# A two-layer trunk kernel: squares of the output projection as tasks of their own, reloads issued in pairs, one table load placed earlier

## The chip, the cores and the metric

The kernel runs on one core of one Trainium2 chip. The metric is the device time of one execution in microseconds (us), as the median of several runs; lower is better. TensorE is called PE here (its weight loads PEld), VectorE DVE, ScalarE ACT, GpSimd POOL and SyncE SP, as in the profile.

## The reference, cut to what matters

Two groups of tokens (128 of context, 512 latent, together T = 640) go through two layers and a closing norm. Each layer normalizes its input, projects it, mixes it in two branches, gates the result, and projects it back with a residual:

```python
for l in range(DEPTH):                      # DEPTH = 2
    shift, scale, gate = modulation(c, ada_w[l], ada_b[l])
    h = rms_norm(x, norm_g[l]) * (1.0 + scale) + shift
    y, side = even_mixer(h, ...) if l % 2 == 0 else odd_mixer(h, ...)
    x = x + gate * (y @ w_out[l])           # the output projection, 2048 x 2048
y_out = rms_norm(x, final_norm_g)           # the closing norm
```

`rms_norm` divides by the root of the mean of `x * x` over the 2048 features. The change is about these squares of the new `x`: their sum over the features is needed by the next layer's norm and by the closing norm.

## The kernel before, in words

**Layout.** Features lie on partitions: `x` is 16 tiles of 128 features by 640 tokens. A projection makes one such tile (a chunk) at a time, in two banks of PSUM (columns 0 to 319 and 320 to 639), with 16 steps over the input features.

**Products in three parts.** Full float32 precision is put together from reduced operands: every input tile is kept as `acth` + `actl`, every weight as `whi` + `wlo`, and PE does whi*acth, whi*actl and wlo*acth (L757). The split of the weights runs while PE works: SP loads raw weights (`wload`, L640), ACT copies them to `whi` (L714), POOL subtracts to get `wlo` (L716; DVE takes every second unit of the last pair of chunks, L715). `whi` and `wlo` are rings of 2560 columns, so a split waits until PE has left the room. `wpump` (L655) emits these steps.

**Strassen pairs.** Most chunks are done two at a time (`spair`, L870) with seven products over six pairs of input tiles and a plain rest. The raw weights come into `rs`, sums of them (S1, S2, S4, S3) are made by DVE into `wraw` and `rs`, and the products run in the order A11, plain, A12, S1, S2, S4, plain, S3, A22 (L596). PE meets the pieces as `acth` or `eh` operands. Folded input sums (`eh`, `el`) and a rewritten half of six `acth`/`actl` tiles serve these products; `unfold` (L1130) reloads the old halves from DRAM (`bh_dram`, `bl_dram`) once a run of Strassen pairs ends, and raises a flag `uf0` to `uf5` for each tile.

**The order of the work** is written by a planner: `Pace` models when each engine would be free; `tick` (L482) is called every few matmuls, emits due DMAs (`dmas`), up to three steps of `wpump`, and advances a list of generator tasks in their order, by default one step a call. A task yields a time, or waits for flags (`wait`), for data in the model (`until`) or until engines' modelled backlog is small (`calm`). `need` moves the model's clock forward by 0.4 us a round until flags are there. All of it fixes only the order in which instructions enter each engine's queue; on the chip an engine runs its queue in order and waits on semaphores.

**The output projection** (`out_proj`, L2409) is done once a layer (l = 0 and 1): chunks n = 0 and 1 as an ordinary pair, n = 2 to 13 as six Strassen pairs, n = 14 and 15 as an ordinary pair (l = 0, `kpair`) or as the closing pair (l = 1, `hpair`, L843, which does columns 0 to 383 of both chunks first, half 0, then columns 384 to 639, half 1). `out_evac` (L1969) takes a finished bank: DVE computes `Y <- bank * G + x` (L1999), and `square` (L1973) then calls `ssq_add` (L1240): ACT squares the half tile into a small buffer, POOL adds that to the running sum `ssq`:

```python
            sq = sq[:, : c.stop - c.start]
            nc.scalar.activation(sq, x[:, c], AF.Square)                      # L1246
            nc.gpsimd.tensor_tensor(ssq[:, c], ssq[:, c], sq, ALU.add)        # L1247
```

In the profile these are `ACT arena<-Y 128x320` and `POOL arena<-arena 128x320`, because `ssq` and the buffers lie in the tile `arena`. The weight splits show as `whi<-rs`, `whi<-wraw`, `wlo<-rs` and `wlo<-wraw`.

**The end.** Before the closing pair a task `reload` (L2638) is started; after `unfold` it reads four pairs of finished output tiles back from DRAM. `final` (L2646) runs after each half of the closing pair: PE sums `ssq` and the last squares over partitions, `rms` (L1220) does Ln and Exp on ACT, DVE finishes the factor, and 16 tiles are scaled and stored, by DVE and, for five of them, by ACT and POOL. Ln and Exp need another ACT table set than the SiLU of the gates; `act` calls `tables` (L524) ahead of the first Ln, and this gives the `ACT_TABLE_LOAD` of L526.

Of the kernel before, what the change touches and what calls it, by code (L numbers as in the profile page):

```python
# [13 lines left out]
AF = mybir.ActivationFunctionType  # L14
ALU = mybir.AluOpType
# [4 lines left out]
KT = D // 128  # L20
# [15 lines left out]
NY = 8  # L36
# [203 lines left out]
class Trunk:  # L240
# [889 lines left out]
    def unfold(self):  # L1130

        nc = self.nc
        for i, j in enumerate(JT):
            for x, y in zip((self.ah, self.al), self.keep):
                self.dma(x[:, j, CW:].bitcast(U32), y[:, j, :].bitcast(U32))
                yield
            self.flags.add(f"uf{i}")
        self.flags.add("unfold")
        self.folded = False
        yield  # L1140
# [828 lines left out]
    def out_evac(self, l, n, f, xsrc, spill):  # L1969
        nc = self.nc  # L1970
        box = {}

        def square(y, c):  # L1973
            if l == 1 and f == KT - 1:
                nc.scalar.activation(self.sq[:, : c.stop - c.start], y[:, c], AF.Square)
            else:
                self.ssq_add(self.ssq, y, f, self.sq if self.cut == CUT else self.sqs.next(), c)

        def squares(y):
            if n == KT - 1:  # L1980
                yield from self.wait("squares")
            for q, s in ((slice(0, HT), self.sqs.next()), (slice(HT, T), self.sqs.next())):
                yield from self.wait("x1:14")
                yield from self.calm(2.0, "a")
                nc.scalar.activation(s, y[:, q], AF.Square)
                yield from self.until(s)
                yield from self.calm(4.0, "v")
                nc.vector.tensor_tensor(self.ssq[:, q], self.ssq[:, q], s, ALU.add)
                yield
            self.flags.add("squares")  # L1990

        def evac(pa, pb):
            G, at = self.G[l], self.cut
            y = self.Y[:, n % NY, :]
            if pa is not None:
                if n < NY:
                    self.clear(f"Y{n}", "C", "R")
                x = box["x"]
                nc.vector.scalar_tensor_tensor(  # L1999
                    y[:, 0:NCTX], pa[:, 0:NCTX], G[:, f, 0:1], x[:, 0:NCTX], ALU.mult, ALU.add  # L2000
                )
                nc.vector.scalar_tensor_tensor(
                    y[:, NCTX:at], pa[:, NCTX:at], G[:, f, 1:2], x[:, NCTX:at], ALU.mult, ALU.add
                )
                if pb is None:
                    square(y, slice(0, at))
            if pb is not None:
                x = box["x"]
                nc.vector.scalar_tensor_tensor(
                    y[:, at:T], pb[:, 0 : T - at], G[:, f, 1:2], x[:, at:T], ALU.mult, ALU.add  # L2010
                )
                if l == 0 or n < NY:
                    self.dma(spill[:, f, :], y)
                if l == 0 and n >= KT - 2:
                    return squares(y)
                if pa is not None:
                    square(y, slice(0, at))
                square(y, slice(at, T))

        def pre():  # L2020
            x = box["x"] = self.xr.next()
            self.dma(x, xsrc[:, f, :])

        return pre, evac
# [144 lines left out]
    def program(self):  # L2169
        nc, tc, d, Y = self.nc, self.tc, self.d, self.Y  # L2170
# [25 lines left out]
        def do(f):  # L2196
            acts.append(("f", f))
# [144 lines left out]
        for kv in range(2):  # L2342
# [26 lines left out]
            for h in range(4 * kv, 4 * kv + 4):  # L2369
                if kv and h != 5:  # L2370
                    i = max(h - 5, 0)
# [37 lines left out]
        def out_proj(l, xsrc, sp):  # L2409
            for i, f in enumerate(range(KT) if l else OUT0):  # L2410
                pre, ev = self.out_evac(l, i, f, xsrc, sp)
                add(wout[l, f], 128, False, pre, ev)
                if i == 1:
                    pair("k", STEPS, f"y{l}", f"uo{l}")
                elif i == KT - 3:
                    pairs((KT - 4) // 2)
# [139 lines left out]
        for i in range(2):  # L2556
            y = lambda i=i: L[f"gy{i}"]
# [3 lines left out]
        for n, i in enumerate(GATES):  # L2561
            y = Y[:, n % NY, :]
# [20 lines left out]
        acts.append(k)  # L2583
        do(lambda: self.need("ada_g1"))
        out_proj(1, spill, ysp)
        do(lambda: self.spawn(self.reload()))
        r = acts.pop()
        pair("h", self.final)
        h = acts.pop()
# [268 lines left out]
```

## Time and profile before

| what | value |
|---|---|
| median of 3 runs | 2102.5 us (2102.18 to 2102.93) |
| the profiled execution | 2104.64 us, of which its span 2102.8 us |
| mean granted TensorE clock in it | 0.996 of full speed |
| layer 0's output projection, Strassen pairs | about 880 to 1040 us of the span |
| layer 1's output projection, Strassen pairs | about 1905 to 2056 us |
| closing pair and closing norm | about 2056 to 2103 us |

The profile is one execution; times in it are counted from its first instruction. A row of the timeline has start, duration, engine, line, operation, `output<-inputs`, shapes, the number of instructions merged into it, and in brackets how long the engine sat idle before it and whose end released it. Nearly every ACT, DVE and POOL instruction is recorded under L214 and every matmul under L397, so the tile names tell them apart. A row of waits has the sum in us, the number of waits and the longest one.

### The profile page before, as it was taken

How to read it: one execution, taken by the hardware profiler on the slowest of the kernel's cores; microseconds unless marked ns; L12 is line 12 of the kernel's file. 1: busy time of each engine (PE TensorE's matmuls, PEld its weight loads, DVE VectorE, ACT ScalarE, POOL GpSimd, SP SyncE). 2: the span in 40 equal slices, each digit the busy share in tenths (PEclk: the TensorE clock that was granted, in tenths of full speed). 3: DMA queues.
4: the chain of work that ended last, by engine and by line, in shares of the span. 5: the costliest groups of instructions: out<-in, count | busy, mean ns of one | idle time of the engine just before them, and what ended most of it. 6: DMA issues, size and time to landing. Idle time of an engine off the chain costs nothing.

```text
span 2102.8 us, 40256 instructions
## 1 busy us (share of the span) xinstructions
PE 2052.0 (98%) x14345; PEld 2000.7 (95%) x14345; DVE 1305.9 (62%) x3034; ACT 1078.3 (51%) x2485; POOL 1301.4 (62%) x1090
## 2 busy tenths in 40 slices
PE   7999999999999999999999999999999999999997
PEld 6899999999999999999999999999999999999996
DVE  4746586676465664787376878787454444466434
ACT  5645565554566866543564434444444544454443
POOL 4656565355455563888755656555655577767884
PEclk9999999999999999999999999999999999999998
DMA  9966343335465544565634454444222344363426
GB/s 362 389 218 207 120 140 123 116 116 175 149 200 173 171 162 149 175 211 181 227 126 129 131 167 152 137 149 148 97 75 94 105 134 131 120 224 116 139 93 240
DMA packets 192841, 340.18 MB, mean 162 GB/s; under 512 B 20896, under 2 KB 70144, under 8 KB 192640
## 3 DMA queue, kind: packets, MB, share of 16 engines
q1 hardware_dynamic: 191296, 336.45, 48.4%
q8 instruction: 112, 1.84, 0.4%
q10 hardware_dynamic: 1344, 1.17, 0.2%
q14 instruction: 89, 0.73, 0.1%
HBM read 303.03 MB, written 31.88 MB: 159 GB/s over the span
## 4 chain that ended last, share of the span: by engine, by line
PE 79%; DMA 7%; DVE 6%; POOL 3%; issue 3%; ACT 2%; SPq 1%; ACTq 0%; POOLq 0%; DVEq 0%
PE bank L397 76%; POOL wlo L214 2%; PE bank L402 2%; DVE arena L214 1%; DVE adas L214 1%; DVE Y L214 1%; DMA adas<-gateT 1%; DMA more<-ada 1%; DVE bank L214 1%; ACT arena L214 1%; DMA Y<-xT 1%; DMA adas<-ada 1%; SPq L431 1%; PE bank L1426 1%; POOL actl L214 0%
## 5 line engine op out<-in xcount | busy, mean ns | idle before, releaser
L397 PE MATMUL bank<-acth,whi 128*128 128x320 f32 (+3 forms) x3320 | 1020.9, 318 | 7.3 <-ACT bc L214 3.0
L397 PE MATMUL bank<-acth,wlo 128*128 128x320 f32 (+3 forms) x3320 | 993.9, 310 | 3.2 <-POOL wlo L214 3.0
L397 PE MATMUL bank<-actl,whi 128*128 128x320 f32 (+3 forms) x3320 | 993.2, 310 | 1.1 <-DMA actl<-bl_dram 1.1
L214 POOL TENSOR_TENSOR wlo<-wraw,whi 128x512 fp32r<-128x512 f32 (+1 forms) x446 | 564.5, 1278 | 388.9 <-ACT whi L214 302.3
L397 PEld LDWEIGHTS bank<-acth,whi 128*128 128x128 f32 (+1 forms) x3320 | 617.1, 189 | 16.2 <-ACT bc L214 4.4
L397 PEld LDWEIGHTS bank<-acth,wlo 128*128 128x128 f32 (+1 forms) x3320 | 617.2, 189 | 4.7 <-POOL wlo L214 4.7
L397 PEld LDWEIGHTS bank<-actl,whi 128*128 128x128 f32 (+1 forms) x3320 | 617.2, 189 | 3.2 <-DMA actl<-bl_dram 1.6
L214 POOL TENSOR_TENSOR wlo<-rs,whi 128x384 fp32r<-128x384 f32 x370 | 409.2, 1125 | 190.8 <-ACT whi L214 154.3
L214 ACT ACTIVATE whi<-wraw 128x512 fp32r<-128x512 f32 (+1 forms) x456 | 260.7, 587 | 93.0 <-PE bank L397 66.4
L214 ACT ACTIVATE whi<-rs 128x384 fp32r<-128x384 f32 x370 | 183.3, 517 | 59.4 <-PE bank L397 51.2
L397 PE MATMUL bank<-eh,wlo 128*128 128x322 f32 (+1 forms) x666 | 206.8, 311 | 2.2 <-POOL wlo L214 2.2
L397 PE MATMUL bank<-eh,whi 128*128 128x322 f32 (+1 forms) x666 | 209.0, 314 | 0.0
L397 PE MATMUL bank<-el,whi 128*128 128x322 f32 (+1 forms) x666 | 206.8, 310 | 0.0
L214 DVE TENSOR_TENSOR wraw<-rs 128x768 f32<-128x768 f32 x74 | 99.1, 1339 | 131.6 <-DMA rs<-w_odd 46.6
L214 POOL TENSOR_TENSOR prod<-adas,mixrow 128x512 f32<-128x512 f32 x94 | 123.6, 1324 | 84.4 <-ACT prod L214 59.1
L214 DVE CUSTOM_DVE_ANT_0 adas<-adas,bank,partg 128x256 bf16<-128x256 f32 (+1 forms) x290 | 156.2, 539 | 12.0 <-DMA adas<-ada_g 4.6
L214 ACT ACTIVATE arena<-arena,bc 128x512 f32<-128x512 f32 (+4 forms) x189 | 97.8, 538 | 76.4 <-DVE arena L214 71.3
L397 PEld LDWEIGHTS bank<-eh,wlo 128*128 128x128 f32 x666 | 125.5, 188 | 3.5 <-POOL wlo L214 3.5
L397 PEld LDWEIGHTS bank<-el,whi 128*128 128x128 f32 x666 | 125.8, 189 | 0.0
L397 PEld LDWEIGHTS bank<-eh,whi 128*128 128x128 f32 x666 | 125.5, 188 | 0.1
L214 DVE TENSOR_TENSOR bank<-bank,sums 128x320 f32<-128x320 f32 (+1 forms) x148 | 70.7, 493 | 72.8 <-PE bank L397 56.3
L214 DVE CUSTOM_DVE_ANT_0 adas<-adas,bank,part 128x512 bf16<-128x512 f32 x142 | 105.6, 744 | 9.5 <-DMA adas<-ada 6.9
(221 smaller groups left out, 2467.7 us busy)
## 6 DMA issues: line engine op xcount, KB each, us to landing
wraw<-w_even SPq DMA_DIRECT2D x176, 256.0 KB, 3.4
adas<-ada_g SPq DMA_DIRECT2D x128, 256.0 KB, 3.6
adas<-ada SPq DMA_DIRECT2D x128, 256.0 KB, 3.6
rs<-w_odd SPq DMA_DIRECT2D x50, 384.0 KB, 3.2
wraw<-w_odd SPq DMA_DIRECT2D x74, 256.0 KB, 3.6
wraw<-w_out SPq DMA_DIRECT2D x60, 256.0 KB, 3.5
rs<-w_odd SPq DMA_DIRECT2D x50, 256.0 KB, 3.9
Y<-ada SPq DMA_DIRECT2D x24, 512.0 KB, 7.7
```

The costliest lines, as they stand in the source:

```text
L214: return f(*args, **kw)
L397: self.nc.tensor.matmul(out, lhsT, rhs, start=start, stop=stop, **kw)
L402: self.nc.tensor.transpose(out, in_, self.ident[:k, :k])
L431: self.nc.sync.dma_start(out, in_)
L1426: nc.tensor.matmul(o, c, w, start=j < 4, stop=j >= 12)
```

## The change

It has three parts. (1) Squares of chunks n = 0 to 11 of both output projections are no longer emitted at the end of the evacuation; each becomes a task (`late`) that follows the one before it (flag `sq{l}:{i}`), waits until the model has the half tile ready and ACT at most 1.0 us behind, emits the square, waits for it and for POOL to be at most 1.5 us behind, and emits the add. Chunks 12 to 15 are squared as before. `need` in `evac` makes sure that a slot of `Y` isn't written again before its squares are emitted, and that all 24 are emitted before chunk 12's evacuation. (2) `unfold` yields once per tile, after both of its DMAs, and not after each DMA. (3) `tables` is called where `reload` is started, ahead of the closing pair.

```diff
@@ unfold
         for i, j in enumerate(JT):
             for x, y in zip((self.ah, self.al), self.keep):
                 self.dma(x[:, j, CW:].bitcast(U32), y[:, j, :].bitcast(U32))
-                yield
             self.flags.add(f"uf{i}")
+            yield
         self.flags.add("unfold")
@@ out_evac
         def square(y, c):
-            if l == 1 and f == KT - 1:
+            if n < KT - 4:
+                self.spawn(late(y, c, 2 * n + (c.start > 0)))
+            elif l == 1 and f == KT - 1:
                 nc.scalar.activation(self.sq[:, : c.stop - c.start], y[:, c], AF.Square)
             else:
                 self.ssq_add(self.ssq, y, f, self.sq if self.cut == CUT else self.sqs.next(), c)
+
+        def late(y, c, i):
+            yield from self.wait("ssq" if i == 0 else f"sq{l}:{i - 1}")
+            yield from self.until(y[:, c])
+            yield from self.calm(1.0, "a")
+            if i < 2:
+                nc.scalar.activation(self.ssq[:, c], y[:, c], AF.Square)
+            else:
+                s = self.sqs.next()
+                nc.scalar.activation(s, y[:, c], AF.Square)
+                yield from self.until(s)
+                yield from self.calm(1.5, "g")
+                nc.gpsimd.tensor_tensor(self.ssq[:, c], self.ssq[:, c], s, ALU.add)
+            self.flags.add(f"sq{l}:{i}")
+            yield
@@ evac
             G, at = self.G[l], self.cut
+            if n >= KT - 4:
+                self.need(f"sq{l}:{2 * KT - 9}")
             y = self.Y[:, n % NY, :]
             if pa is not None:
                 if n < NY:
                     self.clear(f"Y{n}", "C", "R")
+                    self.flags.add("ssq")
+                else:
+                    self.need(f"sq{l}:{min(2 * (n - NY) + 1, 2 * KT - 9)}")
                 x = box["x"]
@@ program
-        do(lambda: self.spawn(self.reload()))
+        do(lambda: [self.tables(), self.spawn(self.reload())])
```

## The prediction, made before the changed kernel was run

> **What bounds the kernel now.** I read the busy row of the page first.
>
> ```profile
> PE 2052.0 (98%) x14345; PEld 2000.7 (95%) x14345; DVE 1305.9 (62%) x3034; ACT 1078.3 (51%) x2485; POOL 1301.4 (62%) x1090
> ```
>
> PE is busy 98% of the span, and the change takes no matmul away. So it can only win where PE stands still, or in the tail after its last matmul. The next view is that of PE's own waits, in the two output projections: first 860 to 985 us, then 1893 to 1925 us (sum, times, longest).
>
> ```profile
> PE bank L397 <- POOL wlo L214: 3.7, 5, 1.0
> ```
>
> ```profile
> PE bank L397 <- POOL wlo L214: 1.1, 1, 1.1
> ```
>
> PE waits here for POOL's half of a weight split, 3.7 + 1.1 = 4.8 us in six stalls; nothing else stops it there. What holds POOL up shows in the timelines of PE, ACT, POOL and DVE around one of the six.
>
> ```profile
> 970.53 0.31 PE L397 MATMUL bank<-acth,whi 128*128 128x320 f32 x1
> 970.68 0.31 PE L397 MATMUL bank<-actl,whi 128*128 128x320 f32 x1
> 971.76 0.41 PE L397 MATMUL bank<-acth,wlo 128*128 128x320 f32 x1 [0.78 <-POOL wlo L214]
> 972.01 0.31 PE L397 MATMUL bank<-acth,whi 128*128 128x320 f32 x1
> ```
>
> ```profile
> 969.32 0.47 ACT L214 ACTIVATE arena<-Y 128x320 f32<-128x320 f32 x1 [5.36 <-DVE Y L214]
> 969.70 0.93 ACT L214 ACTIVATE whi<-rs 128x384 fp32r<-128x384 f32 x2
> ```
>
> ```profile
> 966.28 2.71 POOL L214 TENSOR_TENSOR wlo<-rs,whi 128x384 fp32r<-128x384 f32 x2
> 969.87 0.88 POOL L214 TENSOR_TENSOR arena<-arena 128x320 f32<-128x320 f32 x1 [0.89 <-PE bank L397]
> 970.70 1.98 POOL L214 TENSOR_TENSOR wlo<-rs,whi 128x384 fp32r<-128x384 f32 x2
> ```
>
> ```profile
> 963.53 0.97 DVE L214 TENSOR_TENSOR rs<-rs 128x768 f32<-128x768 f32 x1
> ```
>
> The raw sum for this split was ready at 964.5, and POOL was free from 966.28 + 2.71 = 968.99 on. But ACT stood 5.36 us at a square, in front of the `whi` copies, until DVE had written `Y`; then POOL did the add (0.88) before the split. So the split started at 970.70 instead of 968.99, 1.7 us late, and PE lost about 1.0. The one stall of layer 1 has the same shape.
>
> ```profile
> 1914.17 0.47 ACT L214 ACTIVATE arena<-Y 128x320 f32<-128x320 f32 x1 [4.51 <-DVE Y L214]
> 1914.72 1.02 POOL L214 TENSOR_TENSOR arena<-arena 128x320 f32<-128x320 f32 x1 [0.89 <-ACT arena L214]
> 1915.70 1.96 POOL L214 TENSOR_TENSOR wlo<-rs,whi 128x384 fp32r<-128x384 f32 x2
> 1916.74 0.43 PE L397 MATMUL bank<-acth,wlo 128*128 128x320 f32 x1 [1.06 <-POOL wlo L214]
> ```
>
> **Part 1, the squares.** A stall costs more than its idle time: in the example the starts are 1.08 and 0.25 us apart where 0.15 (970.53 to 970.68) is usual, so 0.93 + 0.10 = 1.03 for an idle 0.78, that is 0.25 more. Six stalls: 4.8 + 6 x 0.25 = 6.3 us. The change puts the squares behind the next `wpump` steps and emits them only once `Y` is there in the model, so ACT no longer stands in front of a ready copy. The gain lies between 0 (the planner emits them where they were) and 6.3 (all six go). I take all six, since in the example the split could come 1.7 us earlier and 1.03 would do.
>
> The 24 squares and adds per layer remain, and they must land somewhere. The grouped rows of 1893 to 2056 us and the busy time of two stretches of layer 0 (PE, PEld, DVE, ACT, POOL) price that.
>
> ```profile
> L214 POOL TENSOR_TENSOR arena<-arena 128x320 f32<-128x320 f32 x24 | 27.7, 1162 | 15.7 <-ACT arena L214 15.7
> ```
>
> ```profile
> 944.00:971.00 27.00, 26.01 (x174) 25.23 (x172) 23.43 (x56) 10.47 (x24) 21.35 (x21) 1.00 0.69 224
> 971.00:998.00 27.00, 26.24 (x179) 26.24 (x180) 19.84 (x40) 11.09 (x26) 24.68 (x23) 1.00 0.41 137
> ```
>
> An add takes 1.16 us, and POOL stood 15.7 us in front of them: time that it now has for splits. But POOL is busy 21.4 to 24.7 of 27 us per Strassen pair, so an add that lands just ahead of a split PE waits for costs its whole length. Between none and one per Strassen pair (12 x 1.16 = 13.9 us) I take one per layer, 2.3 us, near the lower end, because the task waits until POOL is within 1.5 us of free. ACT hides the squares: it is busy about 11 of 27 us. A square still holds its slot of `Y` and the next square; the new `need` queues nothing on an engine, it only moves the model's clock.
>
> **Part 2, the paired reloads.** In the closing pair PE waits twice for a reloaded `actl` half; the last of the six is issued late on SP's queue.
>
> ```profile
> 2068.09 0.44 PE L397 MATMUL bank<-actl,whi 128*128 128x384 f32 x1 [0.42 <-DMA actl<-bl_dram]
> 2069.61 0.45 PE L397 MATMUL bank<-actl,whi 128*128 128x384 f32 x1 [0.64 <-DMA actl<-bl_dram]
> ```
>
> ```profile
> 2057.96 0.43 SPq L431 DMA_DIRECT2D actl<-bl_dram  x1
> 2060.06 0.33 SPq L431 DMA_DIRECT2D wraw<-w_out  x1
> ...
> 2065.40 0.32 SPq L431 DMA_DIRECT2D actl<-bl_dram  x1
> ```
>
> ```profile
> actl<-bl_dram SPq DMA_DIRECT2D x6, 160.0 KB, 4.1
> ```
>
> One task step per DMA put the last `actl` at 2065.40, behind weight loads; landing takes 4.1 us, and PE had it at 2069.6. Now six steps issue all twelve. The sixth step so far is the `actl` of 2057.96; with six more issues of 0.43 in front, the last one goes at about 2060.5 and lands at about 2064.6 (estimates from these rows), 4 us before PE wants it. Both stalls go: 0.42 + 0.64 + 2 x 0.25 = 1.6 us. Moved behind them are weight loads and, as `unfold` ends sooner, the four reads of `reload` (640 KB each); they may pass the last weight loads, whose splits come after 2076, with 6 us to spare. If that cover were gone, PE would lose what it gains here, 1.6. The two earlier `unfold`s cost nothing: PE has no wait row there.
>
> **Part 3, the table load.**
>
> ```profile
> 2076.42 0.63 ACT L214 ACTIVATE whi<-wraw 128x512 fp32r<-128x512 f32 x1 [0.59 <-PE bank L397]
> 2077.07 1.28 ACT L526 ACT_TABLE_LOAD   x1
> 2078.36 0.58 ACT L214 ACTIVATE rstd<-bank,eps 128x384 f32<-128x384 f32 x1
> ```
>
> It stands in the middle of half 0's norm, 1.28 us. What follows is late by as much, and PE and the last square meet it in half 1:
>
> ```profile
> 2084.93 0.38 PE L397 MATMUL bank<-acth,wlo 128*128 128x256 f32 x1 [0.41 <-POOL wlo L214]
> 2089.12 0.70 PE L397 MATMUL bank<-arena,ones 128*128 128x256 f32 x2 [0.24 <-ACT arena L214]
> ```
>
> ```profile
> 2087.23 1.54 ACT L214 ACTIVATE Y<-Y,small 128x640 f32<-128x640 f32 x2
> 2088.67 0.40 ACT L214 ACTIVATE arena<-Y 128x256 f32<-128x256 f32 x1
> ```
>
> The stall of 0.41 (0.66 with its restart) goes, and about 0.35 of the last square's wait behind the two scalings of 1.54. The bounds are 0 and 1.28; I take 1.0, as beyond it PE's last chunk ends the half. At its new place the load delays the next `whi` copies by 1.28. The split with the least room there is DVE's:
>
> ```profile
> 2058.76 1.28 DVE L214 TENSOR_TENSOR wlo<-wraw,whi 128x512 fp32r<-128x512 f32 x1 [1.12 <-ACT whi L214]
> ```
>
> ```profile
> 2062.43 0.33 PE L397 MATMUL bank<-acth,wlo 128*128 128x384 f32 x1
> ```
>
> It ends at 2060.04 and PE first wants it at 2062.43: 2.39 us of cover, so 1.28 costs nothing. Without it PE would lose the 1.28.
>
> The Trainium skill (ScalarE: Activation LUTs, "What ACT_TABLE_LOAD costs") prices a switch at 1.28 us for the load plus 1.38 us for a drain, 2.66 together. Here the Ln starts 0.01 us after the load ends and the load 0.02 after the copy, so the trace agrees with the load and shows no drain. By the page's figure the cover of 2.39 would fall 0.27 short.
>
> **The sum.** 6.3 - 2.3 + 1.6 + 1.0 = 6.6 us. The profiled execution took 2104.64 with a span of 2102.8; the median of the runs is 2102.5, so the difference is taken from the median: 2102.5 - 6.6 = **2095.9 us**.
>
> **The rivals.** *The stalls come back elsewhere.* All emission after layer 0's first evacuation is planned anew, and POOL has little room in layer 0. If part 1 nets nothing, 1.6 + 1.0 = 2.6 remain: 2099.9. For it speaks that two adds in a row can be slow, in POOL's timeline of layer 1:
>
> ```profile
> 2006.66 3.02 POOL L214 TENSOR_TENSOR arena<-arena 128x320 f32<-128x320 f32 x2 [1.20 <-ACT arena L214]
> 2015.49 0.88 POOL L214 TENSOR_TENSOR arena<-arena 128x320 f32<-128x320 f32 x1 [0.21 <-ACT arena L214]
> ```
>
> that is 1.51 each against 0.88; against it, that layer 1 lives with that without a stall. The Trainium skill (SBUF — State Buffer, "Who interferes with whom") says that a DVE instruction with two SBUF inputs and a GpSimd one that reads SBUF exclude each other; the two durations fit it, and at 1.51 per add my 2.3 would be 3.0.
>
> *The squares pile up (slower).* The tasks wait for POOL to be nearly idle; if the model rarely sees that, chunk 12's `need` emits the rest at once: after the needs of n = 8 to 11 up to 16 adds. In POOL's queue they stand before the next splits, which in layer 1 have about 3.0 us of room (two adds, 3.02, in one go cost PE nothing above). Ten adds in each layer cost 2 x (11.6 - 3.0) = 17.2, less 8.9 for the full gains: 2110.8. It turns slower from seven adds on (2 x (8.1 - 3.0) = 10.2). Against it: POOL's 15.7 us of waiting in layer 1 become free.
>
> *The table rule holds.* By mechanism: the load's neighbours are held 2.66 us, DVE's split comes 0.27 late, PE loses 0.27 + 0.25 = 0.5: 2096.4. The rows speak against it.
>
> *It doesn't do what it says.* If `need` brings the squares out at once, order and part 1 stay: 2099.9 as in the first rival.
>
> **How the numbers follow.** A measurement of this kernel can tell about 0.2%, 4.2 us, from no change: faster is below 2098.3, slower above 2106.7. The forecast gets 0.60 and the table rule 0.03, both faster: 0.63. Stalls elsewhere get 0.20 and no change of order 0.05, both within: 0.25. The pile-up gets 0.12. The range of the forecast alone goes from all gains without the 2.3 (2102.5 - 8.9 = 2093.6) to 2098.3; as PE's losses in the six stalls are worked out from one of them, I go to 2092.0 below, and to 2104.0 above, which takes in the first rival with some loss of its own and leaves out the pile-up.
>
> **What would show it.** Part 1 right: PE's wait rows for `wlo` at 880 to 985 and 1905 to 1920 us gone, ACT's long idle times before `arena<-Y` (5.36 and 4.51 above) cut to a fraction, POOL no longer idle before its adds. Wrong: new `wlo` waits of PE, above all before chunk 12. Part 2: no PE wait for `actl<-bl_dram`, and the `acth`, `actl` issues next to each other. Part 3: the table load near 2058, the Ln right behind the sum, no `wlo` wait in half 1. The prediction fails if the planner's new order makes a wait that no row here shows.

## The result, and the profile after

The changed kernel takes 2095.7 us (median of 14 runs, 2093.9 to 2100.2) against 2101.9 (14 runs, 2100.2 to 2107.2) for the kernel before on the same chip. The ratio is 0.9972, 95% interval 0.9964 to 0.9980. The forecast was 2095.9. The profiled execution has a span of 2094.3 us against 2102.8.

The first view is the one that the prediction read first, PE's own waits, here of the changed kernel from 860 to 2075 us, which holds both output projections and the closing pair's reloads (sum, times, longest):

```profile
PE bank L397 <- POOL wlo L214: 1.0, 2, 0.5
PE bank L397 <- ACT Y L214: 0.6, 2, 0.3
PE bank L397 <- ACT whi L214: 0.3, 1, 0.3
```

The kernel before has 4.8 us in six waits for `wlo` here, and 1.1 in two for `actl`. The six are gone, the two are gone, but two new waits for `wlo` and one for `whi` have come. The two for `Y` lie outside the parts that the change touches (at 1379 and 1473 us); the kernel with part 1 alone, below, has none.

The grouped rows of layer 1's projection (busy, mean ns, then idle time ahead and what ended it) show that the squares moved as meant. The first is of the kernel before (1893 to 2056 us), the other two of the changed kernel (1888 to 2050 us):

```profile
L214 ACT ACTIVATE arena<-Y 128x320 f32<-128x320 f32 x26 | 12.2, 472 | 46.1 <-DVE Y L214 45.8
...
L214 ACT ACTIVATE arena<-Y 128x320 f32<-128x320 f32 x26 | 12.1, 466 | 14.9 <-DVE Y L214 14.6 <-POOL arena L214 0.3
L214 POOL TENSOR_TENSOR arena<-arena 128x320 f32<-128x320 f32 x24 | 23.1, 963 | 4.8 <-ACT arena L214 4.6
```

ACT's idle time ahead of its squares fell from 46.1 to 14.9 us, POOL's ahead of its adds from 15.7 to 4.8, and an add from 1162 to 963 ns. The new waits of PE are read in the timelines of PE, ACT, POOL and DVE, in this order, around the first two of them:

```profile
886.55 0.41 PE L397 MATMUL bank<-acth,whi 128*128 128x320 f32 x1 [0.29 <-ACT whi L214]
887.63 0.41 PE L397 MATMUL bank<-acth,wlo 128*128 128x320 f32 x1 [0.52 <-POOL wlo L214]
...
885.65 0.44 ACT L214 ACTIVATE acth<-bank 128x320 fp32r<-128x320 f32 x1 [4.86 <-DVE bank L214]
885.98 0.93 ACT L214 ACTIVATE whi<-rs 128x384 fp32r<-128x384 f32 x2
...
886.58 1.98 POOL L214 TENSOR_TENSOR wlo<-rs,whi 128x384 fp32r<-128x384 f32 x2 [2.39 <-ACT whi L214]
...
885.12 0.50 DVE L214 TENSOR_TENSOR bank<-bank,actl 128x320 f32<-128x320 f32 x1
```

It is the shape of before, with another instruction in front. ACT stood 4.86 us at `acth<-bank`, the copy with which the task `fold` writes a folded tile back, until DVE had the last of three sums in the bank (885.12 + 0.50). Behind it stood the `whi` copies, and POOL, idle for 2.39 us, had nothing to split. No square and no add is near. Layer 1 has the same once, in PE, ACT and POOL:

```profile
1909.08 0.41 PE L397 MATMUL bank<-eh,wlo 128*128 128x320 f32 x1 [0.45 <-POOL wlo L214]
...
1907.09 0.44 ACT L214 ACTIVATE acth<-bank 128x320 fp32r<-128x320 f32 x1 [4.35 <-DVE bank L214]
1907.42 1.34 ACT L214 ACTIVATE whi<-rs 128x384 fp32r<-128x384 f32 x3
...
1908.02 3.67 POOL L214 TENSOR_TENSOR wlo<-rs,whi 128x384 fp32r<-128x384 f32 x3 [1.17 <-ACT whi L214]
```

Part 2 shows in SP's queue of the changed kernel. The pairs stand together, and the last one is issued ahead of the weight loads:

```profile
2052.54 0.38 SPq L431 DMA_DIRECT2D acth<-bh_dram  x1
2052.96 0.43 SPq L431 DMA_DIRECT2D actl<-bl_dram  x1
2054.30 0.32 SPq L431 DMA_DIRECT2D acth<-bh_dram  x1
2054.70 0.40 SPq L431 DMA_DIRECT2D actl<-bl_dram  x1
...
2056.24 1.39 SPq L431 DMA_DIRECT2D wraw<-w_out  x3
```

Part 3 shows on ACT, and what is left of the tail behind it on PE:

```profile
2052.26 1.28 ACT L526 ACT_TABLE_LOAD   x1
2053.56 2.20 ACT L214 ACTIVATE whi<-wraw 128x512 fp32r<-128x512 f32 x4
...
2069.54 0.58 ACT L214 ACTIVATE rstd<-bank,eps 128x384 f32<-128x384 f32 x1
...
2080.62 0.70 PE L397 MATMUL bank<-arena,ones 128*128 128x256 f32 x2 [0.23 <-ACT arena L214]
```

**How the gain is told apart by stage.** PE runs the same matmuls in the same order in every kernel here, so the start of the n-th PE row of one trace can be set against the n-th of another. The difference grows where PE is faster and shrinks where it is slower, and the steps around a stall, with the smaller ones of its restart, are its whole price. The table gives what PE gained on the kernel before in each stage, from its first row on, by the times of before (us; the experiments are told below; layer 0 is 882 to 989, layer 1 is 1900 to 1926, reloads 2052 to 2070, tail 2070 to 2089):

```
kernel         0-882  layer 0  989-1900  layer 1  reloads  tail
changed         3.64     3.01     -1.10     0.25     1.69  0.85
after_again     1.12     2.91     -0.56     0.25     1.69  0.84
two_tables      2.68     2.56     -0.01     0.27     1.69  0.85
p1_squares     -1.35     2.42      0.00     0.28    -0.22  0.01
p2_pairs        0.42     0.21     -0.07     0.01     1.69  0.01
p3_table        4.98     0.53     -0.02     0.07    -1.06  0.86
no_squares      2.66     3.67     -0.58     0.25     1.69  0.84
square_early    4.56     3.83     -0.01     0.27     1.69  0.85
add_behind      3.98     3.41     -0.04     0.24     1.69  0.85
fold_until      1.00     3.86     -0.01     1.92     1.69  0.85
fold_early      5.22     3.87     -2.17     1.92     1.69  0.85
fold_free       2.89     5.19     -0.04     1.92     1.69  0.85
two_switch      3.32     3.09     -0.57     0.23     1.69  0.85
```

The first column is no gain of any kernel: up to there the code is that of before, and the first three rows are one and the same program, 1.1 to 3.6. The last two columns repeat to 0.01. Layer 0 repeats to about 0.5 (2.56 to 3.09 for the first three and `two_switch`, which are one program up to 2052 us, and 0.2 and 0.5 for `p2_pairs` and `p3_table`, which change nothing there). So the change itself is worth 3.0 + 0.25 + 1.7 + 0.85 = 5.8 us in this trace, against 5.9 for the ratio of 0.9972.

### The profile page after: what moved, and what is told of

The parts are those of the page before. It is cut to its first block, busy times and chain, and to the rows that moved or that the text cites. A ratio compares the mean times of both kernels' runs of the same rounds, so it can differ in the third digit from the quotient of the medians.

```text
span 2094.3 us, 40283 instructions
## 1 busy us (share of the span) xinstructions
PE 2049.8 (98%) x14345; PEld 1998.8 (95%) x14345; DVE 1312.7 (63%) x3034; ACT 1080.9 (52%) x2485; POOL 1294.5 (62%) x1090
## 5 line engine op out<-in xcount | busy, mean ns | idle before, releaser
L214 POOL TENSOR_TENSOR wlo<-wraw,whi 128x512 fp32r<-128x512 f32 (+1 forms) x446 | 570.8, 1290 | 423.6 <-ACT whi L214 336.1
L214 POOL TENSOR_TENSOR wlo<-rs,whi 128x384 fp32r<-128x384 f32 x370 | 404.2, 1109 | 203.4 <-ACT whi L214 158.4
```

The costliest lines, as they stand in the source:

```text
L214: return f(*args, **kw)
```

## The experiments

**The parts by themselves.** Each kernel is the one before with one part of the diff. The theory was that the three parts add up.

`p1_squares`: the tasks `late` and the two `need`s alone.

> The squares as tasks alone; reloads and table load as before. If the gain comes from ACT no longer standing at a square ahead of ready weight copies, PE's waits for wlo in the two output projections fall from 4.8 us to about 1.3 (what the whole change left there), while both actl waits (1.1 us) and the wlo wait of the last half (0.4) stay: about 3.5 us faster than before, ratio about 0.9983. If instead the parts only work together, nothing is gained: ratio 1.000.

Measured: 2098.2 us (10 runs) against 2102.2, ratio 0.9984 (0.9974 to 0.9994), so 3.4 us; by PE's starts 2.4 + 0.3 - 0.2 = 2.5. PE's waits, 860 to 2075 us:

```profile
PE bank L397 <- DMA actl<-bl_dram: 1.3, 2, 0.7
PE bank L397 <- POOL wlo L214: 1.2, 3, 0.5
PE bank L397 <- ACT whi L214: 0.3, 1, 0.3
```

The new `whi` and `wlo` waits are here already, so they belong to part 1; the two `actl` waits are those of before, 0.2 us longer in this execution, and that is the loss of 0.22 at the reloads.

`p2_pairs`: the `yield` in `unfold` moved behind both DMAs, alone.

> The paired reloads alone. PE's two actl waits go (1.1 us idle, 1.6 with restarts), its wlo waits in the output projections stay at about 4.8: 1.6 us faster, ratio about 0.9992, which times can hardly tell from 1.000; the trace must tell it. The rival is that the weight loads moved behind the reloads come late: then an ACT wait for wraw turns into a new wlo wait of PE in the closing pair, and the gain is gone.

Measured: 2101.3 us (10 runs), ratio 0.9999 (0.9989 to 1.0010). The time alone can't show a gain of this size. The trace does: the `actl` waits are gone, PE gains 1.69 us at the reloads and nothing elsewhere beyond what identical code differs by. Its one row of PE waits in 860 to 2075 us:

```profile
PE bank L397 <- POOL wlo L214: 4.7, 6, 1.1
```

`p3_table`: `self.tables()` ahead of `reload`, alone.

> The table load alone. The Ln of half 0 starts within 0.3 us of PE's sum and the wlo wait of 0.41 near the end is gone: 1.0 us faster, ratio about 0.9995, to be told by the trace. At the new place the load must cost PE nothing, as the nearest split has 2.39 us to spare. The rival, a switch that takes 2.66 us, makes a PE wait of about 0.3 us in half 0 of the closing pair.

Measured: 2103.1 us (10 runs), ratio 1.0006 (0.9996 to 1.0017). By PE's starts the tail gains 0.86, but the reloads lose 1.06, so the expectation that the load costs PE nothing fell. PE's waits there are more and longer than before; they are followed by SP's, DVE's and ACT's timelines, in this order:

```profile
2062.32 0.44 PE L397 MATMUL bank<-acth,whi 128*128 128x384 f32 x1 [0.48 <-DMA acth<-bh_dram]
2063.84 0.44 PE L397 MATMUL bank<-acth,whi 128*128 128x384 f32 x1 [0.46 <-DMA acth<-bh_dram]
2064.93 0.44 PE L397 MATMUL bank<-actl,whi 128*128 128x384 f32 x1 [0.66 <-DMA actl<-bl_dram]
...
2055.16 0.33 SPq L431 DMA_DIRECT2D wraw<-w_out  x1
2055.59 0.38 SPq L431 DMA_DIRECT2D acth<-bh_dram  x1
...
2054.45 0.69 DVE L214 TENSOR_TENSOR wlo<-wraw,whi 128x512 fp32r<-128x512 f32 x1 [2.54 <-ACT whi L214]
...
2052.48 1.28 ACT L526 ACT_TABLE_LOAD   x1
2053.78 2.20 ACT L214 ACTIVATE whi<-wraw 128x512 fp32r<-128x512 f32 x4
```

Read from below: the load delays the `whi` copies, these DVE's split, which ends at 2055.14, and SP issues its next weight load 0.02 us later, because that load overwrites what the split reads (the queue's own waits show 2.0 us behind DVE's `wlo` there). The reloads stand behind that weight load in SP's queue. In the kernel before the same pair is 2058.76 + 1.28 = 2060.04 and 2060.06; PE is there 5.74 us later than in this trace, so the queue moved on at 2054.32 on this trace's clock, 0.84 us sooner. PE does not feel the late split; it feels the late reloads. In the changed kernel all pairs but the last are issued ahead of 2053.4, and the load costs nothing.

**What is left: the squares or something else?** `no_squares` is the changed kernel without the squares and adds of chunks 1 to 11 (chunk 0's remain, so its sums of squares leave those chunks out).

```diff
-            else:
-                s = self.sqs.next()
-                nc.scalar.activation(s, y[:, c], AF.Square)
-                ...
-                nc.gpsimd.tensor_tensor(self.ssq[:, c], self.ssq[:, c], s, ALU.add)
```

> The changed kernel with the squares and adds of chunks 1 to 11 of both projections left out (the sums of squares are therefore incomplete), which bounds what any placing of them can bring. If the waits that the change left (0.29 and 0.52 us in layer 0, 0.45 in layer 1) come from adds that landed ahead of a split, as the prediction had it, they go: about 2 us faster than the changed kernel. If they come from ACT standing at the copies of the rewritten input half (4.86 and 4.35 us idle there), they stay, and the time is that of the changed kernel within 0.5 us.

Measured: 2094.8 us (8 runs), ratio 0.9969 (0.9958 to 0.9979). Layer 0 gains 3.67 instead of 3.01, layer 1 the same 0.25, and the new waits stand as they were:

```profile
PE bank L397 <- POOL wlo L214: 1.0, 2, 0.5
PE bank L397 <- ACT whi L214: 0.3, 1, 0.3
```

So squares and adds are not what stops PE at 887 and 1909 us. They do cost PE 0.7 us in layer 0, in two steps of its starts, at 972 and 975 us by the times of before. POOL and PE of the changed kernel at the second of them:

```profile
965.43 0.88 POOL L214 TENSOR_TENSOR arena<-arena 128x320 f32<-128x320 f32 x1
966.28 3.23 POOL L214 TENSOR_TENSOR wlo<-wraw,whi 128x512 fp32r<-128x512 f32 x3
...
967.61 0.41 PE L397 MATMUL bank<-acth,wlo 128*128 128x320 f32 x1
```

An add stands ahead of three splits. The first of them, of 512 columns, takes about 1.29 us (as the same split alone does in `square_early`), so it ends near 967.57, and PE starts 0.04 later, 0.45 behind its row before where 0.15 is usual. In `no_squares` neither step is there. This is the prediction's give-back, an add ahead of a split that PE waits for, but in layer 0 alone and at 0.7 us, not at 2.3.

`after_again` is the changed kernel again. `two_tables` asked for a second load of the same table set; its trace has one load only, so it is the same program once more.

> The changed kernel once more, beside the next ones on the same chip. Expected: 5.5 to 6.5 us below the kernel before (ratio 0.9970 to 0.9974). PE's wait rows in 800 to 2103 us as in its first trace: POOL wlo about 1.0 in two stalls, ACT whi 0.3. The steps of PE's starts that the parts account for should repeat: about 2.8 us in layer 0's Strassen pairs, 0.25 in layer 1, 1.7 at the closing pair's reloads, 0.85 in the tail. What PE gained at the start of the span (3.8 us) and lost near 1379 and 1473 us (1.1) should not repeat, if it is difference from run to run.

> The changed kernel with a second table load right behind the first. If the load's price is its 1.28 us on ACT alone, two rows of 1.28 stand side by side, the four whi copies come 1.28 later, DVE's first split ends near 2056.2 where PE wants it near 2055.95, and PE loses about 0.25 to 0.5 us there and nothing else; all reloaded pairs but the last are issued already, so no DMA wait comes back. If each load holds ACT for 2.66 us (load and drain), the whi copies come 2.7 us or more later than in the changed kernel and PE loses about 1.6 to 1.9 us there. If the reloads are behind the splits after all, waits of bank<-acth or bank<-actl for DMA return, as with the table load alone (0.4 to 0.7 each).

Measured: 2096.6 (5 runs), ratio 0.9969 (0.9957 to 0.9981), and 2096.6 (5 runs), ratio 0.9967 (0.9955 to 0.9979). The stage gains repeat as the table shows. The first stage's 3.6 and the loss of 1.1 between 989 and 1900 us do not, so they are differences between executions. As `two_tables` came out as the changed kernel, what its expectation says of a second load stands untested by it; `two_switch` below takes it up.

**The theory of the fold copy.** `fold_until` is the changed kernel with one more line in `fold`: the copy is emitted only once DVE's sum is there in the model.

```diff
                 sub(q, q, f32(h))
                 sub(q, q, f32(l))
+                yield from self.until(q)
                 yield from split(h, l, q)
```

> The changed kernel with one more line: the task that writes the last part of the folded tiles back (its first half is ACT's copy acth<-bank, the copy that ACT stood at for 4.86 us in layer 0 and 4.35 us in layer 1) emits that copy only once DVE's sum is there in the model. My theory (the remaining stalls come from ACT standing in order at this copy, in front of whi copies that are ready): the stalls of 0.29 and 0.52 us near 887 us and of 0.45 near 1909 go, and PE's starts gain about 0.8 + 0.5 = 1.3 us in layer 0 and 0.7 in layer 1, so about 2.0 us below the changed kernel (ratio to before about 0.996). Rival (the adds or the splits fill POOL there, whoever stands where): the three stalls stay, no gain. Second rival (the copy comes later and the tiles' readers wait for it): new PE waits for acth or actl, up to 2 us lost.

Measured: 2093.4 us (6 runs), ratio 0.9951 (0.9939 to 0.9964), against 2096.6 for the changed kernel on the same chip. All three waits are gone. By PE's starts it gains 0.85 in layer 0 and 1.67 in layer 1 on the changed kernel, 2.5 where 2.0 was expected. That the three waits go shows their cause. The 0.85 is made of three things: the waits near 887 us that go (1.9), the steps at 972 and 975 us that are not there either (0.7), and one new wait (1.7 lost). The new wait in PE and then ACT:

```profile
897.90 0.41 PE L397 MATMUL bank<-acth,whi 128*128 128x320 f32 x1 [1.09 <-ACT acth L214]
...
893.06 0.82 ACT L214 ACTIVATE arena<-Y 128x320 f32<-128x320 f32 x2
897.05 0.47 ACT L214 ACTIVATE arena<-Y 128x320 f32<-128x320 f32 x1 [3.17 <-POOL arena L214]
897.43 0.42 ACT L214 ACTIVATE acth<-bank 128x320 fp32r<-128x320 f32 x1
```

The third square in a row needs a scratch buffer, there are two, and ACT stood 3.17 us until POOL's add had freed one. The fold's copy, now behind it, came too late. `fold_free` adds the model's wait for that buffer:

```diff
                 s = self.sqs.next()
+                while (t := self.pace.ready("a", [self.pace.span(s)], []) - self.now) > 0:
+                    yield t
                 nc.scalar.activation(s, y[:, c], AF.Square)
```

> The kernel with the waiting fold copy (fold_until), and one more wait in the model: a late square is emitted only once POOL's add has freed its scratch buffer. In fold_until ACT stood 3.17 us at a square for that buffer, and the fold's copy of acth behind it came 1.09 us late for PE, near 897 us. My theory (ACT works in order, so whatever stands first and waits delays what PE needs behind it): that stall and its restarts (1.25 + 0.38 = 1.6 us by the starts of PE) go, nothing else changes: 1.6 us below fold_until, about 10 us below the kernel before (ratio about 0.9945 to 0.995). Rival (the copy is late because its task is advanced late, not because of the square): the stall stays, the time is that of fold_until within 0.5 us.

Measured: 2092.4 us (5 runs), ratio 0.9954 (0.9940 to 0.9968). The stall is gone, and layer 0 gains 1.33 us on `fold_until` (1.6 expected). Between 870 and 2050 us PE has one wait of its own left:

```profile
PE bank L397 <- DVE actl L214: 0.2, 1, 0.2
```

By PE's starts this kernel has 5.19 + 1.92 + 1.69 + 0.85 = 9.7 us on the kernel before. In the times the intervals of `fold_until` and `fold_free` overlap almost wholly, so that the last step helps is shown by the trace, not by the times. The interval of either lies wholly below 1, and either is faster than the changed kernel by its median and by PE's starts (2.5 and 3.9 us).

**Does the late emission matter, or only the place?** `square_early` is the changed kernel without the waits of the model ahead of a square:

```diff
         def late(y, c, i):
             yield from self.wait("ssq" if i == 0 else f"sq{l}:{i - 1}")
-            yield from self.until(y[:, c])
-            yield from self.calm(1.0, "a")
```

> The changed kernel, but the late squares no longer wait in the model for their Y nor for ACT to be nearly idle: they are still tasks behind the next weight steps, only emitted early. My theory (what part 1 wins is that ACT no longer stands at a square whose Y is not there): ACT's idle time in front of arena<-Y in layer 1 goes from 14.6 back towards 46, and some of PE's wlo stalls return, so 1 to 3 us are lost against the changed kernel. Rival (being a later task is enough, the waits in the model add nothing): ACT's idle time and the time stay as in the changed kernel.

Measured: 2094.7 us (4 runs), ratio 0.9957 (0.9944 to 0.9970). My expectation fell. ACT does stand longer at squares again; the grouped rows of layer 0 (860 to 998 us) of the changed kernel, with the fold copies that are needed further down, and then the squares of this one:

```profile
L214 ACT ACTIVATE arena<-Y 128x320 f32<-128x320 f32 x22 | 10.2, 462 | 8.5 <-DVE Y L214 5.7 <-POOL arena L214 2.7
...
L214 ACT ACTIVATE acth<-bank 128x320 fp32r<-128x320 f32 x6 | 2.6, 439 | 16.6 <-DVE bank L214 14.0 <-DVE Y L214 2.7
```

```profile
L214 ACT ACTIVATE arena<-Y 128x320 f32<-128x320 f32 x22 | 10.1, 464 | 25.1 <-DVE Y L214 21.0 <-POOL arena L214 4.2
```

25.1 us of standing against 8.5 (in layer 1, of which the expectation spoke, 20.6 us behind DVE's `Y` against 14.6, and 45.8 before the change), and PE lost nothing; layer 0 even gained 0.8 more. Of that, 0.7 are the two steps at 972 and 975 us: here POOL does the split first and the add behind it. Standing by itself costs nothing, and being a later task, behind the next weight steps, was enough here. Why it was enough is not shown: at 955.02 us of this trace ACT stood 6.40 us at a square with `whi` copies behind it, and POOL was idle for 5.17 us until the first of them was done, and PE met no wait even so. `fold_early` does the same to `fold_until`:

> The kernel with the waiting fold copy, and the late squares emitted early (without the waits for Y and for ACT, as in square_early). If it matters only where squares stand against the whi copies, this gives what fold_until and square_early gave together: about 0.5 to 1 us below fold_until. If an instruction that stands on ACT delays the fold copies behind it, ACT's idle time before squares of layer 0 (6.4 us in fold_until, 21.0 in square_early) grows and PE's waits for acth near 890 to 900 us grow with it: 1 to 3 us above fold_until.

Measured: 2094.1 us (4 runs), ratio 0.9957 (0.9943 to 0.9971). By PE's starts it is level with `fold_until` up to 989 us and then loses 1.5 us in one step. PE, ACT and POOL there:

```profile
987.35 0.41 PE L397 MATMUL bank<-eh,wlo 128*128 128x320 f32 x1 [1.33 <-POOL wlo L214]
...
979.98 0.47 ACT L214 ACTIVATE arena<-Y 128x320 f32<-128x320 f32 x1 [6.53 <-DVE Y L214]
980.36 0.51 ACT L214 ACTIVATE whi<-wraw 128x384 fp32r<-128x384 f32 x1
...
981.00 2.13 POOL L214 TENSOR_TENSOR wlo<-wraw,whi 128x384 fp32r<-128x384 f32 x2 [4.10 <-ACT whi L214]
983.09 2.54 POOL L214 TENSOR_TENSOR arena<-arena 128x320 f32<-128x320 f32 x2
985.59 4.64 POOL L214 TENSOR_TENSOR wlo<-rs,whi 128x384 fp32r<-128x384 f32 x4
```

Here is the stall of the kernel before once more: a square that stands 6.53 us, a `whi` copy behind it, POOL idle for 4.10, and then two adds (2.54) ahead of the split that PE waits for. The waits for `acth`, which I expected to grow, stayed at 1.1, as the one behind the scratch buffer does not hang on `Y`. So the model's wait is no gain of its own here; at most it keeps an emission from landing in front of a ready copy that PE needs soon, and for that this one place is the only evidence.

**Two sizes.** `add_behind` is the changed kernel with the add emitted right behind its square:

```diff
                 nc.scalar.activation(s, y[:, c], AF.Square)
-                yield from self.until(s)
-                yield from self.calm(1.5, "g")
                 nc.gpsimd.tensor_tensor(self.ssq[:, c], self.ssq[:, c], s, ALU.add)
```

> The changed kernel, but POOL's add is emitted right behind its square, without waiting for the square's end or for POOL to be nearly idle. My theory (the add's place costs PE little, as leaving all squares and adds out gave at most 1.5 us): within 1 us of the changed kernel, with POOL standing a little longer in front of its adds. Rival (an add just ahead of a split that PE waits for costs its 1.0 us each time, as the prediction had it): more wlo waits of PE, 2 to 6 us above the changed kernel.

Measured: 2095.9 us (6 runs), ratio 0.9968 (0.9957 to 0.9980), with the same two `wlo` waits of 1.0 in all. Emitting the add sooner costs PE no more: layer 0 gains 3.41. The steps at 972 and 975 us are gone, and one of 0.3 at 916 us is new, again at a split right behind an add. So an add ahead of a split costs PE some tenths of a microsecond where it hits, not its whole length.

`two_switch` loads another table set right ahead of the changed kernel's load:

```diff
-        do(lambda: [self.tables(), self.spawn(self.reload())])
+        do(lambda: [self.tc.nc.scalar.preload_act_table_set("exp_and_others"), self.tables(), self.spawn(self.reload())])
```

> The changed kernel with a load of another table set right ahead of its table load (the second load of the same set was dropped in the program, so that run was the changed kernel once more). If the price of a load is its 1.28 us on ACT and no more, two rows of 1.28 stand side by side, the whi copies come 1.28 later, DVE's first split ends near 2056.2 where PE wants it near 2055.95, and PE loses 0.25 to 0.5 us there. If a switch holds ACT for 2.66 us, the copies come 2.7 later and PE loses 1.6 to 1.9. All reloaded pairs but the last are issued ahead of the splits, so no DMA wait comes back; if the reloads hang on the splits all the same, waits of 0.4 to 0.7 for acth or actl return as with the table load alone.

Measured: 2096.5 us (8 runs), ratio 0.9975 (0.9965 to 0.9985). ACT's timeline:

```profile
2052.54 1.28 ACT L2608 ACT_TABLE_LOAD   x1
2053.83 1.28 ACT L526 ACT_TABLE_LOAD   x1
2055.13 2.20 ACT L214 ACTIVATE whi<-wraw 128x512 fp32r<-128x512 f32 x4
```

Each load takes its 1.28 us, the next instruction starts 0.01 to 0.02 later, and PE has no wait from 2040 to 2075 us: the gain at the reloads is the same 1.69. The small loss that I expected from the late split did not come: it ends at 2056.48, and the PE row that the prediction took for its first reader starts at 2056.75 in this trace. I had placed that row at 2055.95, too early.

## Why the prediction came true, step by step

The time was right to 0.2 us, in part by luck: the forecast took 6.6 us off a median of 2102.5, while the change is worth 5.8 to 5.9 and the kernel before came out at 2101.9 in the longer series. By PE's starts two of the three parts were right in size and cause. Two steps failed in their mechanism: the give-back of part 1, whose size was right by luck, and the cover of part 3.

- **Part 1, the stalls (6.3 us).** Right. By PE's starts the changed kernel wins 4.6 us in layer 0 (1.18 at 889, 0.44 at 912, 0.94 at 918, 0.28 at 945, 1.02 at 965, 0.76 at 972, by the times of before) and 1.2 in layer 1 (0.24 and 0.96): 5.8. These are the steps of 0.2 us and more; the restarts of about 0.1 behind most of them are left out, here and in the next point. With the fold copy out of the way it is 5.2 + 1.9 = 7.1 net. The cause was right as well: `fold_early` brings it back in one place. Wrong in it was that the squares must wait for `Y`; that they are later tasks was enough in `square_early`.
- **The give-back (2.3 us, "one add per layer ahead of a split").** This step failed. What came back is 2.6 us, and 2.3 of it did not come through adds: 1.4 in layer 0 (0.25, 0.46 and 0.68 near 887 us) and 0.9 in layer 1 (0.28 and 0.61 near 1909). `no_squares` and `add_behind` leave these waits as they are, and `fold_until` removes them. That this is just the 2.3 of the forecast is chance. An add ahead of a split, which the forecast meant, brought back the 0.30 at 975 us, kept another 0.3 of the stall at 972, and cost nothing in layer 1. What stops PE near 887 and 1909 us is ACT in order: the instruction at the head of its queue had only changed its name. The kernel before shows it in its other ACT instructions with a long idle time ahead. In layer 0 (860 to 998 us):

```profile
L214 ACT ACTIVATE acth<-bank 128x320 fp32r<-128x320 f32 x6 | 2.6, 439 | 11.1 <-DVE bank L214 7.8 <-DVE Y L214 3.3
```

  After the change ACT stands 16.6 us ahead of these six (the second row of layer 0 above). The wait that the squares used to hold moved to the next instruction that was emitted before its input was there.
- **Part 2 (1.6 us).** Right: 1.69 in every kernel with the paired reloads, the stalls gone, the issues adjacent. The weight loads that moved behind them cost no PE wait.
- **Part 3 (1.0 us, "1.28 costs nothing").** The gain was 0.85: 0.67 for the stall of 0.41, as forecast, and 0.18 at PE's sum over the squares ahead of the last one, while PE's wait for the last square, which was to bring 0.35, stayed (0.24 before, 0.23 after). The cover was right only together with part 2. I compared the late split with PE's first use of it and found 2.39 us of room; the nearer reader is SP's queue, whose next weight load waits for that split with reloads behind it. Alone, the load costs 1.06 there and part 3 nets -0.2.
- **The table rule as a rival.** The Trainium skill (ScalarE: Activation LUTs, "What ACT_TABLE_LOAD costs") puts a drain of 1.38 us beside the load at every switch to a different set. `two_switch` shows two loads and the next copy 0.01 and 0.02 us apart, so no such time shows here.
- **The other rivals.** The squares did not pile up: no `wlo` wait stands ahead of chunk 12's evacuation. "Stalls come back elsewhere" came true for 2.6 of 5.8 us.

What stays open: why being a later task is enough in `square_early` although copies still stand behind squares there, and why one program differs by 0.5 us in layer 0. A part of the latter shows: `two_tables`, `two_switch` and `p1_squares` lose 0.4 to 0.5 us at 969 us (by the times of before), where PE again starts as a split right behind an add ends; the first two executions of the changed kernel, with the same order on POOL, do not.

## What to carry to other kernels

When an in-order engine stands at an instruction whose input is late, moving that instruction uncovers the next one like it: list every group of that engine by its idle time, look at what is ready behind each, and mend them together. An instruction that stands costs nothing if nothing that is needed soon is behind it. For a delay on one engine, ask who else waits for the delayed result: here a DMA queue, with transfers behind it, needed it sooner than the matmuls did.

## What the runs showed of the hardware that I had not expected

Identical code differs from one execution to the next by several us in the first 882 us of the span. PE's n-th start there moved from -1.4 to +5.2 us against the same matmul of the kernel before, with no change of the program up to that point; from 2052 us on the gains of all kernels with the whole change agree within 0.02. Waits for DMAs repeat less well: `p1_squares`, with SP's queue there in the order of before, lost 0.22 more at the same two. A gain of 1 to 2 us is seen in the aligned starts of PE here, not in the medians of ten runs.
